# The feed-forward's down products read their activations in nine interleaved column orders

## The chip, the cores and the metric

The kernel runs on one core of a Trainium2 chip. The metric is the device time of one execution in microseconds (us). The engines are TensorE (PE in the profile; PEld is its weight load), VectorE (DVE), ScalarE (ACT), GpSimd (POOL) and SyncE (SP), which issues most DMAs. SBUF is the on-chip memory, PSUM the banks into which TensorE accumulates.

## The reference

A two-layer encoder over 512 positions of width 1024: each layer adds a mixer (attention heads in layer 0, an mLSTM in layer 1), a cross-attention to a memory, and a gated feed-forward with a short causal convolution. What bears on the change is the feed-forward:

```
def conv_ffn(xn, w_up, conv_w, conv_b, w_down):
    h = causal_depthwise_conv(xn @ w_up, conv_w) + conv_b
    g, u = jnp.split(h, 2, axis=-1)
    return (jax.nn.gelu(g) * u) @ w_down          # w_down: 2816 x 1024

x = x + conv_ffn(rms_norm(x, ffn_norm[layer]), ...)
```

Everything is float32.

## The kernel before, in words

x is kept transposed: eight tiles `x[m]` of 128 features x 512 positions, 4 bytes an element. A product with a weight matrix is cut into 128 x 128 weight blocks that are held in TensorE, past which the 512 columns (positions) of an activation tile are streamed. To keep float32 precision every operand is split into two fp32r parts, high and low, and each block is three matmuls, in `mm3` (lines 287 to 292): high by high (line 290), the activation's low part by the high weights (291), the high part by the low weights (292). So one "k" of a product is three weight loads and three matmuls of 512 columns. The first argument of `mm` after the bank is the held operand, the second the streamed one; in the profile's names the streamed one stands first behind the arrow (`w<-ah,wh` streams `ah` past weights of `wh`).

The feed-forward is `ffn_steps` (from line 1247). 2816 = 22 x 128 features go in 22 steps, "pairs" (gate and up half of one block): the first four as plain products (`plain`), the other 18 as seven products of half width (`seven`), in 256 columns. `tail` forms gate times up, and splits it into the activation tiles `acts[p]` = (`ah`, `al`), each 128 x 512, of which ten buffers exist. The down product is cut along its input features into five chunks, `CHUNKS`, of 4, 4, 4, 4 and 6 tiles (line 24). For chunk c and output block m, `down(c, m)` (line 1557) calls `block` (line 1310): it loads the weights, ScalarE and VectorE split them, TensorE runs 4 (or 6) times `mm3` into one of the two PSUM banks `w`, and VectorE adds the bank to `x[m]` (`xadd`, lines 615 to 618). So one block of chunks 0 to 3 is 12 matmuls, one of chunk 4 is 18. `block` also serves the plain up products, whose operand is `own` (line 1326).

The chunks' blocks are not run in one go: from pair 5 on, each pair calls `fill` twice, and each call takes one waiting block of down products. The last five blocks of chunk 3, and in layer 0 all of chunk 4, come after the last pair. In layer 1 chunk 4 is not run by `down` but in `finish` (line 1834), which does the final norm with it.

What order the instructions take on each engine is decided when the program is built, by `Sched`: every piece is added with an engine, an assumed duration, what it depends on, a due time and the buffers it takes (`raw`, `dr`: raw weights; `h`: split weights; `act`: ten activation tiles; `w`: two PSUM banks), and `Sched.run` places them. A `down` block is added to TensorE with 0.7 us for each k, its sum to VectorE with 0.6 us and 3 us later. The engines then run their fixed queues and wait for each other by semaphores.

The few lines that the change's steps touch, in `block` and in `down`:

```
for k in range(c * per, (c + 1) * per):
    self.mm3(st["ps"][:], *st["rows"](k), *xs(k), k == 0, k == nk - 1)
...
lambda k: tuple(a[:] for a in acts[first + k])
...
e = add("DVE", 0.6, lambda: self.xadd(m, d["ps"]), [last, xadded[m], *formed], clock[0] + 3.0, (), [("w", d)])
```

Of the kernel before, what the change touches and what calls it, by code (L numbers as in the profile page):

```python
# [13 lines left out]
ALU = mybir.AluOpType  # L14
# [50 lines left out]
class Plan:  # L65
# [11 lines left out]
    def add(self, fn, dur=0.0, deps=(), prio=None, take=(), free=(), chain=(), pre=(), after=0.0, order=(), load=(), st=None):  # L77
        it = Item(fn, dur, [d for d in deps if d is not None], len(self.items) if prio is None else prio, take, free, chain, pre, after, order, load, st)
        it.n = len(self.items)
        self.items.append(it)  # L80
        return it
# [67 lines left out]
class Sched:  # L149
# [22 lines left out]
    def run(self):  # L172
        order = sorted(self.tasks, key=lambda t: (t.prio, t.n))
        todo = {}
        want = {r: [] for r in self.slots}
        for t in order:
            todo.setdefault(t.eng, []).append(t)
        for t in self.tasks:
            for r, _ in t.take:
                want[r].append(t)  # L180
        now = {e: 0.0 for e in todo}
        inf = float("inf")
        idle = 0.0
        done = []
        while any(todo.values()):
            best = None
            for e, ts in todo.items():
                soon, pick = inf, None
                for t in ts[:120]:
                    at = 0.0 if e == "-" else now[e]  # L190
                    ok = True
                    for d in t.deps:
                        if d.end is None:
                            ok = False
                            break
                        at = max(at, d.end + (0.0 if d.eng == e else d.lat))
                    if not ok:
                        continue
                    for r, _ in t.take:
                        if want[r][0] is not t:  # L200
                            ok = False
                            break
                        at = max(at, self.slots[r][self.slot(r)])
                    if not ok or at == inf:
                        continue
                    if at < soon - 1e-6:
                        soon, pick = at, t
                if pick is not None and (best is None or soon < best[0]):
                    best = (soon, e, pick)
            assert best is not None, [(e, t.n, t.prio, [d.n for d in t.deps if d.end is None], t.take) for e, ts in todo.items() for t in ts[:3]]  # L210
            at, e, t = best
            todo[e].remove(t)
            if e == "PE":
                idle += at - now[e]
            t.start, t.end = at, at + t.dur
            now[e] = t.end
            for r, st in t.take:
                want[r].pop(0)
                s = self.slot(r)
                self.turn[r] += 1  # L220
                self.slots[r][s] = inf
                st["_" + r] = s
            for r, st in t.free:
                self.slots[r][st["_" + r]] = t.end + 0.1
            done.append(t)
        self.now, self.idle = now, idle
        products = [t for t in done if t.eng == "PE"]
        for a, b in zip(products, products[1:]):
            if a.block is not None and b.narrow:
                a.block["apart"] = a.block["step"]  # L230
        for t in done:
            if t.fn:
                t.fn()


class Builder:
# [185 lines left out]
    def xs(self):  # L422
        return self.xh, self.xl
# [188 lines left out]
            self.gained(k, self.x[k][:], self.col(gain, gi * 8 + k), self.xh[k][:], self.xl[k][:])  # L612
        self.squares(k, self.x[k][:], SEQ, state)

    def xadd(self, m, ps, reload=False):
        if reload:
            self.nc.sync.dma_start(self.x[m][:], self.t["x"][m])
        self.nc.vector.tensor_tensor(out=self.x[m][:], in0=ps[:], in1=self.x[m][:], op=ALU.add)  # L618


    def constants(self):
# [625 lines left out]
    def ffn_steps(self, layer, mp):  # L1247
# [3 lines left out]
        nc, t = self.nc, self.t  # L1251
        sc = Sched(raw=3, h=3, s2=1, s4=1, a22=1, sa=3, sb=2, ra=1, hs=2, c=1, dr=2, v=1, u2=1, u3=1, act=10, acc=4, s=2, w=2)
        add = sc.add
# [3 lines left out]
        clock = [0.0]  # L1257
        state = {}
        acts, acted = {}, {}
# [3 lines left out]
        def pe(dur, fn, deps, take=(), free=()):  # L1263
            clock[0] += dur
            return add("PE", dur, fn, deps, clock[0] - dur, take, free, 0.2)

        def joined(deps, prio, free):
            return add("-", 0.0, None, deps, prio, (), free, 0.0)
# [18 lines left out]
        def weight(src, cols, at, tag="raw", off=0):  # L1287

            st = {"apart": 0}
            l = load(st, tag, src, cols, at - 9.0)  # L1290

            def hi():
                st["wh"], st["wl"] = (self.til(self.wp, i, (P, 1088), F32R, bufs=3)[:, off:] for i in ("wh", "wl"))
                nc.scalar.copy(st["wh"][:, :cols], st[tag][:, :cols])  # L1294

            def low():
                n, end = st["apart"], cols - P
                for a, b, c in ((0, end, 0), (end, cols, n)) if n else ((0, cols, 0),):
                    self.sub(st["wl"][:, a + c : b + c], st[tag][:, a:b], st["wh"][:, a:b])

            def rows(k):
                s, n = slice(k * P, (k + 1) * P), k * P + (st["apart"] if (k + 1) * P == cols else 0)
                return st["wh"][:, s], st["wl"][:, n : n + P]

            st["rows"] = rows
            h = add("ACT", act(cols), hi, [l], at - 3.0, [("h", st)])
            lo = add("DVE", tt(cols), low, [h], at - 2.0, (), [(tag, st)])
            return st, lo

        def block(src, nk, xs, at, bank, deps, steps, tag="raw", off=0):  # L1310

            st, lo = weight(src, nk * P, at, tag, off)
            last = None
            per = nk // steps
            for c in range(steps):

                def fn(c=c):
                    if c == 0:
                        st["ps"] = self.acc_bank(st["_acc"]) if bank == "acc" else self.bank(bank)
                    for k in range(c * per, (c + 1) * per):  # L1320
                        self.mm3(st["ps"][:], *st["rows"](k), *xs(k), k == 0, k == nk - 1)

                last = pe(0.7 * per, fn, [lo, last, *deps], [(bank, st)] if c == 0 else (), [("h", st)] if c == steps - 1 else ())
            return st, last
# [33 lines left out]
        formed = []  # L1358
# [195 lines left out]
        xadded = [None] * 8  # L1554
        queue, late = [], []

        def down(c, m, steps=1):
            first, nk = CHUNKS[c]
            d, last = block(
                t[f"down{c}"][layer, m], nk, lambda k: tuple(a[:] for a in acts[first + k]), clock[0], "w", [acted[first + k] for k in range(nk)], steps,  # L1560
                "dr" if nk == 4 else "raw", OFF,
            )
            last.block, d["step"] = d, 16
            if m == 7:
                for k in range(nk):
                    joined([last], last.prio, [("act", acted[first + k].st)])
            e = add("DVE", 0.6, lambda: self.xadd(m, d["ps"]), [last, xadded[m], *formed], clock[0] + 3.0, (), [("w", d)])
            xadded[m] = e
            return e

        def fill():
            nonlocal queue
            if queue:
                down(*queue.pop(0))
# [15 lines left out]
        if layer == 0:  # L1590
            for m in range(8):
                e = down(4, m, 2)
                a = add("ACT", 1.2, lambda m=m: self.xprep(m, "mix", 1, state), [e], clock[0] + 3.0)
                add("DVE", 1.3, None, [a], clock[0] + 3.0)
# [419 lines left out]
```

## Time and profile before

| what | value |
|---|---|
| time, median of 2 runs | 1471.14 us (1469.96 to 1472.32) |
| profiled execution, first to last instruction (span) | 1468.1 us, 3.0 us under the median of the runs; it has no time of its own beside the span |
| TensorE busy | 1455.4 us, 99% |
| VectorE busy | 1225.7 us, 83% |
| ScalarE busy | 843.8 us, 57% |
| bytes moved by DMA | 179.15 MB, mean 122 GB/s |
| matmuls of the down products that the change touches (`w<-ah` and `w<-al`) | 3 x 304 |
| their sums into x (line 618, `x<-w,x`) | 72 |

How to read it: the page lists for each engine how long it was busy, then how busy it was along the span, then the chain of work that ended last, then groups of instructions by source line (line, engine, operation, tiles, shape, count, then busy us and mean ns of one, then idle time before them). A row of the view of busy time by window has, after the window's bounds and length, the busy time and the count of instructions for each engine, the granted TensorE clock, the DMA engines' busy share and GB/s. A row of the timeline has the start and the duration in us, the engine, line, operation, tiles, shape and count. A matmul's duration runs from its start until its last result is out, so matmuls overlap, and the step from one start to the next is the time that it occupies TensorE.

The down products lie at 467 to 747 us in layer 0 and at 1177 to 1424 us in layer 1.

### The profile page before, as it was taken

What the parts mean: (1) busy time and instruction counts of PE and PEld (TensorE: products, weight loads), DVE (VectorE), ACT (ScalarE), POOL (GpSimd) and SP (SyncE); (2) the same over time, 40 slices, a digit from 0 to 9 for tenths busy, and PEclk for the clock granted to TensorE, in tenths of its full rate; (3) what the DMA queues carried; (4) which work ended last, traced back from release to release, by engine and by line L of the source; (5) the groups of instructions that cost most, each with busy time, mean ns of one, the idle gap of its engine ahead of it and who ended that gap; (6) DMA issues with size and microseconds to landing.
All of it is one profiled execution on the core that took longest, in us unless ns stands there. A gap on an engine that the chain in (4) does not pass through costs nothing.

```text
span 1468.1 us, 22621 instructions
## 1 busy us (share of the span) xinstructions
PE 1455.4 (99%) x8503; PEld 1268.9 (86%) x8503; DVE 1225.7 (83%) x2246; ACT 843.8 (57%) x1425; POOL 63.1 (4%) x102
## 2 busy tenths in 40 slices
PE   9999999999999999999999999999999999999998
PEld 7888787888888999999888888888888899999987
DVE  7789985756589999999769988676557999999984
ACT  7788664544466555555457655354445655555554
POOL 0001120000000000000000100000000000000000
PEclk9999999999999999999999999999999999999999
DMA  5222433323237666562333332332323756655422
GB/s 198 87 73 73 122 120 118 115 92 109 86 130 194 166 156 168 157 159 76 92 99 108 115 101 76 119 102 99 115 87 115 191 156 163 161 165 153 118 67 77
DMA packets 64798, 179.15 MB, mean 122 GB/s; under 512 B 7072, under 2 KB 7072, under 8 KB 64688
## 3 DMA queue, kind: packets, MB, share of 16 engines
q1 hardware_dynamic: 58496, 157.71, 33.4%
q0 software_dynamic: 5184, 18.88, 7.7%
q8 instruction: 66, 1.08, 0.3%
q10 hardware_dynamic: 1008, 1.12, 0.2%
q14 instruction: 44, 0.36, 0.1%
HBM read 175.55 MB, written 2.13 MB: 121 GB/s over the span
## 4 chain that ended last, share of the span: by engine, by line
PE 78%; DVE 15%; ACT 3%; issue 2%; DMA 1%; SPq 0%; POOL 0%; ACTq 0%; DVEq 0%; POOLq 0%
PE acc L290 15%; PE acc L291 15%; PE acc L292 15%; PE w L292 5%; PE w L290 5%; PE w L291 5%; DVE wl L281 3%; PE s L290 2%; PE s L292 2%; PE s L291 2%; DVE c L1404 2%; PE acc L351 2%; PE acc L353 2%; PE acc L352 2%; DVE x L770 1%
## 5 line engine op out<-in xcount | busy, mean ns | idle before, releaser
L290 PE MATMUL acc<-xh,wh 128*128 128x512 f32 (+1 forms) x800 | 281.9, 352 | 0.1
L292 PE MATMUL acc<-xh,wl 128*128 128x512 f32 (+1 forms) x800 | 280.0, 350 | 1.1 <-DVE wl L281 1.1
L291 PE MATMUL acc<-xl,wh 128*128 128x512 f32 (+1 forms) x800 | 279.5, 349 | 0.0
L281 DVE TENSOR_TENSOR wl<-raw,wh 128x1024 fp32r<-128x1024 f32 (+4 forms) x199 | 235.7, 1185 | 27.1 <-ACT wh L284 22.9
L284 ACT CAST wh<-raw 128x1024 fp32r<-128x1024 f32 (+1 forms) x135 | 139.3, 1036 | 142.4 <-PE acc L291 89.8
L292 PEld LDWEIGHTS acc<-xh,wl 128*128 128x128 f32 x800 | 150.2, 188 | 22.2 <-DVE wl L281 2.0
L290 PEld LDWEIGHTS acc<-xh,wh 128*128 128x128 f32 x800 | 150.2, 188 | 20.2 <-ACT v L1643 0.6
L291 PEld LDWEIGHTS acc<-xl,wh 128*128 128x128 f32 x800 | 150.3, 188 | 19.7
L1404 DVE SCALAR_TENSOR_TENSOR c<-hs,vec,c 128x512 f32<-128x512 f32 x176 | 129.7, 743 | 0.9 <-ACT c L1397 0.8
L292 PE MATMUL w<-ah,wl 128*128 128x512 f32 x304 | 119.0, 391 | 0.0
L290 PE MATMUL w<-ah,wh 128*128 128x512 f32 x304 | 118.6, 390 | 0.0
L291 PE MATMUL w<-al,wh 128*128 128x512 f32 x304 | 118.6, 390 | 0.0
L1397 ACT ACTIVATE c<-hs,vec 128x512 f32<-128x512 f32 x88 | 69.4, 812 | 47.6 <-DVE hs L1547 34.6
L1294 ACT CAST wh<-dr 128x512 fp32r<-128x512 f32 x64 | 39.6, 619 | 55.7 <-PE w L291 20.5
L292 PEld LDWEIGHTS w<-ah,wl 128*128 128x128 f32 x304 | 57.1, 188 | 12.2
L290 PEld LDWEIGHTS w<-ah,wh 128*128 128x128 f32 x304 | 57.1, 188 | 10.4 <-ACT ah L1418 0.6
L291 PEld LDWEIGHTS w<-al,wh 128*128 128x128 f32 x304 | 57.1, 188 | 9.6
L618 DVE TENSOR_TENSOR x<-acc,x 128x512 f32<-128x512 f32 x32 | 22.0, 691 | 49.3 <-PE acc L292 49.3
L290 PE MATMUL acc<-mem,wh 128*128 128x256 f32 (+1 forms) x192 | 61.2, 319 | 0.0
L291 PE MATMUL acc<-mem,wh 128*128 128x256 f32 (+1 forms) x192 | 61.0, 318 | 0.0
L292 PE MATMUL acc<-mem,wl 128*128 128x256 f32 (+1 forms) x192 | 60.8, 317 | 0.0
L618 DVE TENSOR_TENSOR x<-w,x 128x512 f32<-128x512 f32 x72 | 49.2, 683 | 11.8 <-PE w L292 11.1
(469 smaller groups left out, 3992.4 us busy)
## 6 DMA issues: line engine op xcount, KB each, us to landing
raw<-in_up_dram SPq DMA_DIRECT2D x52, 512.0 KB, 3.3
sa<-in_up_dram SPq DMA_DIRECT2D x36, 512.0 KB, 4.4
sa<-in_up_dram POOLq DMA_DIRECT2D x36, 512.0 KB, 5.5
dr<-in_down_dram SPq DMA_DIRECT2D x64, 256.0 KB, 2.9
ra<-in_up_dram SPq DMA_DIRECT2D x36, 256.0 KB, 3.1
raw<-in_xk_dram SPq DMA_DIRECT2D x16, 512.0 KB, 3.4
raw<-in_wo_dram SPq DMA_DIRECT2D x16, 512.0 KB, 3.3
raw<-in_xq_dram SPq DMA_DIRECT2D x16, 512.0 KB, 3.3
```

What stands on the lines that cost most here:

```text
L281: self.nc.vector.tensor_tensor(out=lo, in0=v, in1=hi.bitcast(F32), op=ALU.subtract)
L284: self.nc.scalar.copy(hi, v)
L290: mm(out, wh, xh, start=first, stop=False, skip_group_check=parts)
L291: mm(out, wh, xl, start=False, stop=False, skip_group_check=parts)
L292: mm(out, wl, xh, start=False, stop=last, skip_group_check=parts)
L351: mm(ps, xh[k][:, ts], wh[:, ws], start=(k == 0), stop=False)
L352: mm(ps, xh[k][:, ts], wl[:, ws], start=False, stop=False)
L353: mm(ps, xl[k][:, ts], wh[:, ws], start=False, stop=(k == 7))
L618: self.nc.vector.tensor_tensor(out=self.x[m][:], in0=ps[:], in1=self.x[m][:], op=ALU.add)
L1294: nc.scalar.copy(st["wh"][:, :cols], st[tag][:, :cols])
L1397: nc.scalar.activation(st["c_"][:, j, :], hs()[:, j, 2:514], AF.Identity, scale=self.col("cw", (layer * 3 + 2) * 44 + blk), bias=self.col( ...
L1404: nc.vector.scalar_tensor_tensor(out=c, in0=hs()[:, j, n : n + 512], scalar=w, in1=c, op0=ALU.mult, op1=ALU.add)
```

## The change

For each layer and chunk an order (h, f) is given. It views the 512 columns as h parts of 512 / h, and streams f neighbouring columns from part 0, f from part 1, and so on through all h parts, then the next f from part 0. (2, 2) for instance streams columns 0, 1, 256, 257, 2, 3, 258, 259, and so on. The bank is written front to back in the order of the stream, so a bank's columns are in that order too. `xadd` reads the bank front to back and reads and writes x in the same interleaved order, so each sum lands where it did. Chunk 4 of layer 1, in `finish`, stays as it was; its entry (None) is not used.

Nine blocks of down products get an order, four or five in each layer:

| layer | chunk 0 | chunk 1 | chunk 2 | chunk 3 | chunk 4 |
|---|---|---|---|---|---|
| 0 | h 2, f 2 | h 2, f 4 | h 2, f 16 | h 4, f 16 | h 2, f 8 |
| 1 | h 8, f 16 | h 16, f 16 | h 4, f 8 | h 16, f 4 | as before |

The instructions of every engine, their order and their waits are the same as before; an operand of 912 matmuls and two operands of 72 additions are described by three steps where it was one.

```
+def woven(h, f):
+    return lambda a: a.rearrange("p (h c f) -> p c h f", h=h, f=f)
+
+ORDERS = [
+    [woven(2, 2), woven(2, 4), woven(2, 16), woven(4, 16), woven(2, 8)],
+    [woven(8, 16), woven(16, 16), woven(4, 8), woven(16, 4), None],
+]
...
-    def xadd(self, m, ps, reload=False):
+    def xadd(self, m, ps, reload=False, order=None):
         if reload:
             self.nc.sync.dma_start(self.x[m][:], self.t["x"][m])
-        self.nc.vector.tensor_tensor(out=self.x[m][:], in0=ps[:], in1=self.x[m][:], op=ALU.add)
+        x, ps = self.x[m][:], ps[:]
+        if order is not None:
+            x = order(x)
+            for n in reversed(x.shape[2:]):
+                ps = ps.rearrange("p (a b) -> p a b", b=n) if len(ps.shape) == 2 else ps.rearrange("p (a b) c -> p a b c", b=n)
+        self.nc.vector.tensor_tensor(out=x, in0=ps, in1=x, op=ALU.add)
...
                     for k in range(c * per, (c + 1) * per):
-                        self.mm3(st["ps"][:], *st["rows"](k), *xs(k), k == 0, k == nk - 1)
+                        x = xs(k)
+                        out = st["ps"][:]
+                        for n in reversed(x[0].shape[2:]):
+                            out = out.rearrange("p (a b) -> p a b", b=n) if len(out.shape) == 2 else out.rearrange("p (a b) c -> p a b c", b=n)
+                        self.mm3(out, *st["rows"](k), *x, k == 0, k == nk - 1)
...
             first, nk = CHUNKS[c]
+            order = ORDERS[layer][c]
             d, last = block(
-                t[f"down{c}"][layer, m], nk, lambda k: tuple(a[:] for a in acts[first + k]), clock[0], "w", [acted[first + k] for k in range(nk)], steps,
+                t[f"down{c}"][layer, m], nk, lambda k: tuple(order(a[:]) for a in acts[first + k]), clock[0], "w", [acted[first + k] for k in range(nk)], steps,
                 "dr" if nk == 4 else "raw", OFF,
             )
...
-            e = add("DVE", 0.6, lambda: self.xadd(m, d["ps"]), [last, xadded[m], *formed], clock[0] + 3.0, (), [("w", d)])
+            e = add("DVE", 0.6, lambda: self.xadd(m, d["ps"], order=order), [last, xadded[m], *formed], clock[0] + 3.0, (), [("w", d)])
```

## The prediction

> **What bounds the kernel now.** I read the page first: the span, the busy shares and the granted clock. Then I read the busy times by window for the feed-forward stages, the waits of TensorE there, and the timeline for the step from one matmul to the next.
>
> ```profile
> span 1468.1 us, 22621 instructions
> PE 1455.4 (99%) x8503; PEld 1268.9 (86%) x8503; DVE 1225.7 (83%) x2246; ACT 843.8 (57%) x1425; POOL 63.1 (4%) x102
> PEclk9999999999999999999999999999999999999999
> PE 78%; DVE 15%; ACT 3%; issue 2%; DMA 1%; SPq 0%; POOL 0%; ACTq 0%; DVEq 0%; POOLq 0%
> ```
>
> TensorE is busy from end to end at the full granted clock. The chain that ended last runs mostly through it. The 15% on VectorE warns that a second engine is close, so I look at the stages that the change touches: 440 to 700 us and 1150 to 1430 us (the pairs of layer 0 and 1, with the early down products between them), and 700 to 760 us (the late down products of layer 0).
>
> ```profile
> core 0: us, PE busy (x) PEld busy (x) DVE busy (x) ACT busy (x) POOL busy (x), PEclk, DMA share, GB/s
> 440.00:700.00 260.00, 259.29 (x1875) 242.27 (x1874) 258.12 (x436) 148.46 (x232) 14.64 (x18) 1.00 0.59 153
> 700.00:760.00 60.00, 59.93 (x275) 49.25 (x274) 43.83 (x66) 28.88 (x42) 0.10 (x1) 1.00 0.31 95
> 1150.00:1430.00 280.00, 279.27 (x1972) 258.86 (x1971) 274.80 (x461) 158.67 (x247) 14.73 (x18) 1.00 0.56 148
> PE acc L290 <- DVE u L1523: 0.2, 1, 0.2
> ```
>
> TensorE is idle for 0.7 us of 260, and the only wait of TensorE's matmuls that the view of waits lists between 460 and 700 us is the last row, 0.2 us. VectorE is idle for 1.9 us of 260 and 5.2 us of 280. So in these stages TensorE ends last and VectorE stands right behind it: time added to a down product has nothing to hide in, and time added to a sum on VectorE has some 7 us at most.
>
> **What one down product costs.** A matmul's duration includes its way through the array; what counts is the step from start to start.
>
> ```profile
> 703.48:747.20 43.72, 43.71 (x192) 35.95 (x193) 7.53 (x11) 0.00 (x0) 1.00 0.30 92
> L290 PE MATMUL w<-ah,wh 128*128 128x512 f32 x304 | 118.6, 390 | 0.0
> L291 PE MATMUL w<-al,wh 128*128 128x512 f32 x304 | 118.6, 390 | 0.0
> L292 PE MATMUL w<-ah,wl 128*128 128x512 f32 x304 | 119.0, 391 | 0.0
> ```
>
> The first row is a window over the tile w: 192 matmuls of the late down products, back to back, in 43.72 us. That is 43.72 / 192 = 0.2277 us for 512 columns, or 0.445 ns a column, although each lasts 0.39. The other rows count the matmuls that change: 3 x 304 = 912, in all 912 x 0.2277 = 208 us of TensorE.
>
> **The change, part by part.** Nothing is added or removed: the same instructions stand on every engine in the same order with the same waits, no DMA moves, and the planner's costs are the same numbers. What differs is one operand of 912 matmuls (the moving one; the output bank is still written front to back) and two operands of 72 sums. An order (h, f) cuts the 512 columns into h equal parts and takes f neighbours from each in turn. So the stream is made of runs of f columns with a jump between them. By run length: runs of 2 in layer 0's chunk 0 (8 blocks x 4 k x 3 = 96 matmuls); of 4 in layer 0's chunk 1 and layer 1's chunk 3 (192); of 8 in layer 0's chunk 4 and layer 1's chunk 2 (144 + 96 = 240); of 16 in the other four (384). Together 912.
>
> *The moving operand.* No matmul of this trace streams a jumping operand, so its price has to be bounded. Lower end: nothing, since 512 columns already go at one steady pace, and no row shows a faster one; for a gain I leave 10 us below (912 x 0.011, a twentieth of the step), because no row excludes that a stream with jumps meets fewer collisions with the weight loads beside it. Upper end: the slowest steady stream of 4-byte columns in the trace, the transposes.
>
> ```profile
> L1215 PE MATMUL w<-ident,xe 128*128 128x128 f32 x64 | 10.5, 272 | 0.0
> 287.57 0.60 PE L1215 MATMUL w<-ident,xe 128*128 128x128 f32 x4
> ```
>
> Four of them take 0.60 us, the last 0.272 of it in flight, so the step is (0.60 - 0.272) / 3 = 0.109 us for 128 columns, 0.855 ns a column. A 512-column product at that pace takes 0.438 us, 0.210 more than now. For all 912 that is +191.5 us.
>
> Between these ends the run length decides. The nearest rows that jump at all are VectorE's, when it forms the gate weights in runs of 4 and 8 columns:
>
> ```profile
> L281 DVE TENSOR_TENSOR wh<-gw,wh 128x32 fp32r<-128x32 f32 x2 | 0.3, 188 | 0.0
> L281 DVE TENSOR_TENSOR wh<-gw,wh 128x64 fp32r<-128x64 f32 x1 | 0.2, 215 | 0.0
> L281 DVE TENSOR_TENSOR wl<-dr,wh 128x128 fp32r<-128x128 f32 x56 | 15.8, 283 | 0.0
> L281 DVE TENSOR_TENSOR al<-c,ah 128x512 fp32r<-128x512 f32 x44 | 30.1, 683 | 0.2
> ```
>
> Without jumps, 128 to 512 columns cost (683 - 283) / 384 = 1.04 ns a column, so 32 would take 183 ns and 64 would take 216. With runs of 4 and 8 they take 188 and 215. So VectorE finds a new run every 4 x 1.04 = 4.2 ns at next to no cost. At TensorE's present pace runs of 16 come every 7.1 ns and runs of 8 every 3.6: about what that row shows, and I take nothing for them. Runs of 4 come every 1.78 ns, runs of 2 every 0.89, beyond what any row shows. If a run can be had as often as a pair of columns in the slow stream (2 x 0.855 = 1.71 ns), runs of 4 just keep pace and runs of 2 fall to 0.855 ns a column. That is my choice: runs of 4 nothing, runs of 2 the upper end, 96 x 0.210 = **+20.2 us**. The ends I keep are 0 and +191.5.
>
> [...]
>
> *The sums.* 72 additions into x read and write x in runs.
>
> ```profile
> L618 DVE TENSOR_TENSOR x<-w,x 128x512 f32<-128x512 f32 x72 | 49.2, 683 | 11.8 <-PE w L292 11.1
> ```
>
> They cost what the contiguous subtraction above costs (683 ns), so they are at the plain pace. Lower end: nothing, as in the gate rows. Upper end: the 5 ns that 8 runs of 4 took too long there, 0.63 ns a run: 8 x 256 + 16 x 128 + 16 x 64 + 32 x 32 = 6144 runs, 3.9 us in all, behind the 7 us that VectorE has idle. I take nothing. If that cover is gone, the 3.9 us go into the span. A sum that ends later frees its w bank later (two banks), which would hold the next but one block.
>
> *What follows a slower product.* In layer 0's chunk 0 (the first 96, from 467.65 us on) each block of 12 takes 2.5 us longer. Behind it on TensorE stand the seven products of a pair; ScalarE and VectorE then wait a little more for banks, but gain the slack that they lack now. DMAs are at 0.59 of the engines' time and ask for nothing more.
>
> **Sum.** 1468.1 + 20.2 = 1488.3 us of span. The runs' median is 1471.14, 3.0 us above the profiled span, so the forecast is **1491 us**, 1.4% slower. A difference of about 2%, or 29 us, is what a measurement of this kernel can tell from no change.
>
> **Rivals.**
> - *No price at all* (1471 us). For: VectorE's gate rows jump free. Against: they run at less than half TensorE's pace. [...]
> - *Every jump costs one column's time*, in the address stepping, whatever the run. Runs: 96 x 256 + 192 x 128 + 240 x 64 + 384 x 32 = 76,800, times 0.445 ns = +34.2 us: 1505, slower by 2.3%, the other side of my forecast. It decides from 0.38 ns a jump on (29.4 us / 76,800). For: TensorE has no slack for it. Against: the 0.63 ns a run of the gate rows, if it is more than scatter, was VectorE's, and 64 columns in runs of 8 showed none.
> - *Runs of 4 pay as well* (start addresses, or two parts that collide): 288 x 0.210 = +60.5 us, 1532.
> - *Any interleaved stream falls to the slow pace*: +191.5, 1663. For: the transposes show that a 4-byte stream can go that slowly. Against: runs of 16 jump every 7 ns only.
> - *The sums pay, not the products*: at twice the plain pace each sum takes 512 x 1.04 = 0.53 us more. Some 59 of them lie in the two full stages, 31 us, less VectorE's 7 us idle: +24, 1495.
> - *A small gain* through fewer collisions: 1461.
>
> **How the numbers follow.** Forecast 0.30, no price 0.25, a price per jump 0.13, runs of 4 too 0.08, everything slow 0.13, sums 0.05, gain 0.06. I predict the likeliest, 1491; its own range is 1483 to 1498, since part of an added 20 us could fall into waits and runs of 2 could be a little better or worse than the transposes. The range is 1460 to 1550: it leaves out the case in which everything is slow (0.13) and some 0.05 of odd outcomes. Slower by over 2%: 0.13 + 0.08 + 0.10 of the price per jump + 0.03 of the forecast's upper tail = 0.34. Faster by over 2%: 0.01, as 29 us of the 208 would need a column in 0.38 ns. Within 2%: 0.65.
>
> **What would show it.** In the changed profile, layer 0's chunk 0 (from 467.65 us on) should have steps of about 0.44 us, and all other down products 0.228; the late ones from about 724 us on should again take 43.7 us for 192. L618's successor should stay at 683 ns. The forecast is wrong if the first 96 step at 0.228 (no price), if steps grow with the number of jumps (0.228 + 0.114, 0.057, 0.028, 0.014 for runs of 2, 4, 8, 16: a price per jump), if runs of 4 or of 16 go at 0.44, or if the sums lengthen.

## The result and the profile after

The changed kernel takes 1489.97 us (median of 2 runs, 1489.52 to 1490.42) against 1471.14 before: a ratio of 1.0129, 95% interval 1.0099 to 1.0158. It is slower, by 1.3%; the forecast was 1491.

The page of the changed kernel, the lines that answer to those shown of before:

```profile
span 1487.5 us, 22621 instructions
PE 1474.9 (99%) x8503; PEld 1272.6 (86%) x8503; DVE 1227.9 (83%) x2246; ACT 843.8 (57%) x1425; POOL 62.4 (4%) x102
PEclk9999999999999999999999999999999999999999
PE 82%; DVE 12%; ACT 3%; issue 2%; DMA 1%; POOL 0%; SPq 0%; ACTq 0%; DVEq 0%; POOLq 0%
L635 DVE TENSOR_TENSOR x<-w,x 128x512 f32<-128x512 f32 x72 | 49.2, 684 | 16.2 <-PE w L304 15.8
```

TensorE's busy time grew by 19.5 us and the span by 19.4. The clock is the same (0.999 in both), VectorE's busy time grew by 2.2 us, and the sums (now line 635) take 684 ns where they took 683. So the time went to TensorE, and the chain shifts from VectorE to it. The busy time by window over the tile w shows where. A row is one block of down products between its first start and the next product's start; first the kernel before, plain order, then the changed one with one block of each order (layer 0's chunks 0 to 3, layer 1's chunks 0 to 3), then the same late 192 matmuls as in the prediction's window.

```profile
471.76:474.50 2.74, 2.74 (x12) 2.07 (x12) 0.68 (x1) 0.00 (x0) 1.00 0.93 215
```

```profile
473.73:477.73 4.00, 4.00 (x12) 2.15 (x12) 0.00 (x0) 0.00 (x0) 1.00 0.11 44
545.79:548.81 3.02, 3.02 (x12) 2.08 (x12) 0.00 (x0) 0.00 (x0) 1.00 0.79 199
602.43:605.31 2.88, 2.88 (x12) 2.09 (x12) 0.00 (x0) 0.00 (x0) 1.00 0.38 124
671.71:674.51 2.80, 2.80 (x12) 2.07 (x12) 0.00 (x0) 0.00 (x0) 1.00 0.97 167
1197.01:1199.87 2.86, 2.86 (x12) 2.08 (x12) 0.68 (x1) 0.00 (x0) 1.00 0.49 138
1270.91:1273.79 2.88, 2.88 (x12) 2.08 (x12) 0.00 (x0) 0.00 (x0) 1.00 0.68 176
1323.33:1326.10 2.77, 2.77 (x12) 2.07 (x12) 0.00 (x0) 0.00 (x0) 1.00 0.65 189
1390.79:1393.74 2.95, 2.95 (x12) 2.11 (x12) 0.00 (x0) 0.00 (x0) 1.00 0.18 65
716.57:762.85 46.28, 46.27 (x192) 36.33 (x193) 7.53 (x11) 0.00 (x0) 1.00 0.29 88
```

Every order costs something, and none costs what the forecast gave it. A plain block takes 2.74 us. The extra time of the one block that is shown, times the eight blocks of its chunk:

| order | run | extra per block, us | chunk, us | forecast, us |
|---|---|---|---|---|
| (2,2) | 2 | 1.26 | 10.1 | 20.2 |
| (2,4), (16,4) | 4 | 0.28, 0.21 | 2.2 + 1.7 | 0 |
| (2,8), (4,8) | 8 | 0.29 (18 matmuls), 0.03 | 2.3 + 0.2 | 0 |
| (2,16), (4,16), (8,16), (16,16) | 16 | 0.14, 0.06, 0.12, 0.14 | 1.1 + 0.5 + 1.0 + 1.1 | 0 |
| all | | | 20.2 | 20.2 |

For (2,8) the late window is used: 46.28 - 43.72 = 2.56 us, less 4 blocks of (4,16), 0.24 us, leaves 2.3 us for its eight blocks. The table goes by one block of each kind; the steps of all 912 matmuls, added up, grew by 19.7 us, 10.1 of it in the runs of 2 and 9.6 in the other eight orders. So the total was met because two errors cancel: runs of 2 pay half of the forecast, the other eight orders pay the other half.

### The profile page after: what moved, and what is told of

Its sections match the earlier page's. It is cut to its first block, busy times and chain, and to the rows that moved or that the text cites. A ratio compares the mean times of both kernels' runs of the same rounds, so it can differ in the third digit from the quotient of the medians.

```text
span 1487.5 us, 22621 instructions
## 1 busy us (share of the span) xinstructions
PE 1474.9 (99%) x8503; PEld 1272.6 (86%) x8503; DVE 1227.9 (83%) x2246; ACT 843.8 (57%) x1425; POOL 62.4 (4%) x102
## 4 chain that ended last, share of the span: by engine, by line
PE 82%; DVE 12%; ACT 3%; issue 2%; DMA 1%; POOL 0%; SPq 0%; ACTq 0%; DVEq 0%; POOLq 0%
PE acc L302 16%; PE acc L303 16%; PE acc L304 16%; PE w L303 6%; PE w L304 6%; PE w L302 6%; PE s L302 3%; PE s L304 3%; PE s L303 3%; DVE wl L293 2%; PE acc L363 2%; PE acc L365 2%; PE acc L364 2%; DVE c L1425 2%; PE w L816 1%
## 5 line engine op out<-in xcount | busy, mean ns | idle before, releaser
L303 PE MATMUL w<-al,wh 128*128 128x512 f32 x304 | 126.1, 415 | 0.0
L304 PE MATMUL w<-ah,wl 128*128 128x512 f32 x304 | 126.0, 414 | 0.0
L302 PE MATMUL w<-ah,wh 128*128 128x512 f32 x304 | 125.8, 414 | 0.0
```

What stands on the lines that cost most here:

```text
L302: mm(out, wh, xh, start=first, stop=False, skip_group_check=parts)
L303: mm(out, wh, xl, start=False, stop=False, skip_group_check=parts)
L304: mm(out, wl, xh, start=False, stop=last, skip_group_check=parts)
```

## The experiments

Theory J, from the table alone, is a fixed slot for each jump (1.26 us / 12 / 256 jumps = 0.41 ns). It fits (2,2), (2,16), (8,16) and (16,16), and fails for runs of 4 and 8. The rivals are named where they come up.

**Eight orders without the first.** Chunk 0 of layer 0 goes back to plain order.

```
-    [woven(2, 2), woven(2, 4), ...
+    [None, woven(2, 4), ...
```

> The changed kernel with layer 0's chunk 0, runs of 2, put back to plain order in products and sums; the other eight orders stay. If the forecast's step was right (runs of 2 carry all of the price) this is the kernel before: 1471 us. If the changed kernel's own steps are right, runs of 2 carry 96 x 0.106 = 10 us and the others the rest: 1480 us.

Measured: 1479.62 us, ratio to before 1.0065 (1.0047 to 1.0083). Runs of 2 carry 1489.97 - 1479.62 = 10.4 us by the medians and 1487.5 - 1477.8 = 9.7 by the profiled spans, and the other eight orders 8 to 10. The forecast's step is wrong, the reading of the blocks right.

**Only the sums.** The products stream in plain order, the sums stay interleaved: layer 0 with the change's orders, layer 1 with single columns. What the layers compute on is thereby permuted.

```
-  lambda k: tuple(order(a[:]) for a in acts[first + k])
+  lambda k: tuple(a[:] for a in acts[first + k])
-    [woven(8, 16), woven(16, 16), woven(4, 8), woven(16, 4), None],
+    [woven(2, 1), woven(256, 1), woven(128, 1), woven(16, 1), None],
```

> Only the sums are interleaved, the products stream their columns front to back as before; so the sums land in permuted columns of x, and the layers compute on permuted sums. Layer 0 has the five orders of the change; layer 1 has single columns: (2,1), (256,1), (128,1), (16,1). If the change's whole price lies in the products: step 0.227 us throughout, layer 0's sums at 0.684 us, the layer 0 part as before. If the sums carry any of it: layer 0's part longer by up to 20 us. [...]

The view of the sums by window, layer 0 whole, then a stretch of layer 1 with (256,1) alone:

```profile
440.00:760.00 320.00, 27.37 (x40) 1.00 0.53 142
1250.00:1300.00 50.00, 4.85 (x7) 1.00 0.63 168
```

40 sums in layer 0's orders take 27.37 us, 0.684 each: free, as forecast. The four orders of layer 1 were not run alone; with products and sums in them, the changed kernel's sums there take 0.684 us. With (256,1), steps of two columns, a sum takes 0.69 us. With the other orders of single columns it takes 1.1 to 1.2 us, where a sum in plain order takes 0.68. The span was 1475.1 us, so 24 dear sums (some 10 us of VectorE) brought 7: VectorE's thin cover in these stages is real.

**The tiles 32 bytes further.** Theory P says that crossing a 64-byte piece of the row costs.

```
+  self.pad(mp, 32)
   act_()
-  self.pad(mp, 192)
+  self.pad(mp, 160)
```

> The changed kernel, with the activation tiles 32 bytes further along in SBUF: as built they start 32 bytes past a multiple of 64, here on one. Theory J (each jump costs the same slot, 0.106 us / 256 = 0.41 ns, wherever it lands): nothing moves, steps stay at 0.333, 0.252, 0.240, 0.233, 0.243 us in layer 0 and 0.238, 0.240, 0.231, 0.246 in layer 1, span 1487.5 us. Theory P (what costs is passing from one 64-byte piece of a row to another; runs of 16 columns are 64 bytes and straddle two pieces as the tiles lie): the four orders with runs of 16 fall to 0.227, that is 96 x (0.013 + 0.006 + 0.011 + 0.013) = 4 us less, span 1483.4, runs of 2, 4 and 8 unchanged. Theory W (the stream collides with the weight loads beside it, by the relative place of the two): prices of all orders change, in no order of run length.

The mean steps stayed: (2,16) 0.240, (4,16) 0.234, (8,16) 0.238, (16,16) 0.240 us, as before the shift. P falls. W is not borne out either: no order's mean step moved by more than 4 ns, and (2,16) later cost 0.240 us in another chunk. The span was 1491.7 us, 4 longer, spread over the pairs of both layers; this is from a single profile, and its cause stays open.

**Other orders, and single columns.**

```
-    [woven(2, 2), woven(2, 4), woven(2, 16), woven(4, 16), woven(2, 8)],
-    [woven(8, 16), woven(16, 16), woven(4, 8), woven(16, 4), None],
+    [woven(4, 2), woven(8, 2), woven(16, 2), woven(4, 4), woven(8, 4)],
+    [woven(8, 8), woven(16, 8), woven(2, 16), woven(2, 2), None],
```

> Other orders in products and sums: layer 0 (4,2), (8,2), (16,2), (4,4), (8,4); layer 1 (8,8), (16,8), (2,16), (2,2). If the price belongs to the order and not to its chunk, (2,2) costs 0.333 and (2,16) 0.240 us a matmul in layer 1 as they did in layer 0. Theory J (run length alone, priced by the change's own rows): all runs of 2 at 0.333, runs of 4 at 0.25, runs of 8 at 0.24; 384 x 0.106 + 240 x 0.025 + 192 x 0.015 + 96 x 0.013 = 51 us, span 1519. Theory D (the distance of the jump counts too; h = 4, 512 bytes, was the cheap one twice): (4,2) and (4,4) at about half the price, 0.28 and 0.237 us, h = 8 and 16 like h = 2; span about 1512.

Blocks of (4,2), (8,2), (16,2), and of (2,2) in layer 1:

```profile
474.79:480.17 5.38, 5.38 (x12) 2.25 (x12) 0.00 (x0) 0.00 (x0) 1.00 0.16 42
573.79:579.69 5.90, 5.90 (x12) 2.28 (x12) 0.00 (x0) 0.00 (x0) 1.00 0.20 48
637.99:643.53 5.54, 5.54 (x12) 2.29 (x12) 0.00 (x0) 0.00 (x0) 1.00 0.48 139
1456.36:1460.36 4.00, 4.00 (x12) 2.14 (x12) 0.00 (x0) 0.00 (x0) 1.00 0.11 13
```

(2,2) takes 4.00 us a block in another layer too: the price belongs to the order, not to its place. But other runs of 2 cost 0.45 to 0.49 us a matmul, about the 0.438 that the forecast had taken from the transposes, and far from J's 0.333. Theory D falls as well: (4,2) and (4,4) take 0.448 and 0.268 us a matmul, where it had 0.28 and 0.237. The span was 1559.9 us.

> Products stream single columns with jumps: layer 0 (2,1), (256,1), (128,1), (64,1), (8,1); layer 1 (32,1), (16,1), (4,1), and (4,16) as a control. The sums are plain, so they land in permuted columns of x. Theory J (0.41 ns a jump): 512 jumps, 0.440 us for every order of single columns, 816 x 0.213 = 174 us, span 1642. [...] A stream limited by fetches, one per run of 2 every 0.333/256 = 1.30 ns: 512 x 1.30 = 0.666 us, 816 x 0.44 = 358 us, span 1826. Control (4,16) 0.233.

The edit is the same with orders of single columns and plain sums. Blocks of (2,1), (256,1), (128,1), (64,1) and (4,1):

```profile
471.36:473.94 2.58, 2.58 (x12) 2.08 (x12) 0.68 (x1) 0.00 (x0) 1.00 1.03 170
550.12:555.54 5.42, 5.42 (x12) 2.27 (x12) 0.00 (x0) 0.00 (x0) 1.00 0.15 58
633.15:638.65 5.50, 5.50 (x12) 2.27 (x12) 0.00 (x0) 0.00 (x0) 1.00 0.47 143
704.16:709.32 5.16, 5.16 (x12) 2.26 (x12) 0.00 (x0) 0.00 (x0) 1.00 0.72 181
1457.35:1460.63 3.28, 3.28 (x12) 2.09 (x12) 0.00 (x0) 0.00 (x0) 1.00 0.26 94
```

This was the surprise of the study, and it ends J: (2,1), with a jump at every column, takes 2.58 us a block, 0.216 a matmul, *less* than plain order. And (256,1), which only steps by two columns, takes 5.42 us, twice as long. The other orders of single columns but (4,1) take 0.430 to 0.487 us a matmul. The control (4,16) stayed at 0.234. The span was 1613.9 us, 28 below J's.

Theory T answers to (2,1) and (256,1). It is about the order alone: call the even places of the stream one lane and the odd places the other; then the pace goes by how each lane steps, not by where the two lie. In (2,1) the even lane walks column by column through the first half and the odd lane through the second: 0.216 us a matmul. In plain order each lane steps by two, 0.227 us, in (256,1) by four, 0.452 us. What in TensorE would do this no row shows.

**Pairs at any distance.** If T holds, how far apart the two lanes walk should not count. The walks leave columns out or take them twice.

```
+def walk(*dims):                      # (step, count) of each loop, the innermost last
+    return lambda a: bass.AP(a.tensor, a.offset, [a.ap[0], *[list(d) for d in dims]])
+def pair_at(d):
+    return walk((1, 256), (d, 2))      # columns c, c + d, c + 1, c + 1 + d, ...
```

> Products stream pairs (column c, column c + d), c = 0 to 255: in layer 0 d = 128, 64, 16, 4, 0; in layer 1 d = 1, then even columns of the first half with odd columns of the second in turn (each lane steps two columns), then d = 252, then d = 256 as in (2,1). Where d is not 256 columns are left out or taken twice, and the sums are plain, so what is computed is not the feed-forward's product; only the steps are read. Theory T (two lanes, each with neighbours): 0.216 us for every d, and about 0.227 for the lanes that step two columns. Theory H (the two places of a pair have to lie 1024 bytes apart, in different halves): 0.216 for d = 256 only, 0.43 to 0.49 like the single columns of the earlier run for d = 128, 64, 16, 4. Theory J (each jump its slot): 0.44 for all.

Blocks with d = 128, then d = 1, then two lanes that step by two columns in different places:

```profile
472.06:474.65 2.59, 2.59 (x12) 2.08 (x12) 0.69 (x1) 0.00 (x0) 1.00 0.73 172
1178.04:1180.63 2.59, 2.59 (x12) 2.08 (x12) 0.68 (x1) 0.00 (x0) 1.00 0.96 164
1256.75:1259.50 2.75, 2.75 (x12) 2.07 (x12) 0.00 (x0) 0.00 (x0) 1.00 0.86 231
```

All distances give 0.216 (0, 4, 16, 64, 252 and 256 too), and two lanes that step by two in different places go at plain order's 0.227. T stands, H and J fall.

**A price by pieces.** Plain order and steps of four suggest a way to count. Cut the row into pieces of four columns: in plain order each lane passes 128 of them, at 0.2267 us / 128 = 1.77 ns a piece, and in (256,1) each passes 256, at 0.452 us / 256, again 1.77 ns. The estimate from these two steps and that of (2,1): a matmul takes the larger of 0.216 us and 1.77 ns times the pieces that one lane passes. With lanes that take r neighbouring columns and then skip r, that is 0.227 us for r = 2 and 0.216 from r = 4 on; with steps of three columns, 192 pieces, 0.340; with steps of six, 256 pieces, 0.453 and not more than with steps of four.

```
+def lanes(r):
+    return walk((2 * r, 256 // r), (1, r), (r, 2))      # each lane r neighbours, then skips r
+ORDERS = [
+    [lanes(2), lanes(4), lanes(8), lanes(32), walk((0, 2), (3, 128), (64, 2))],
+    [walk((0, 4), (6, 64), (64, 2)), walk((0, 2), (2, 128), (0, 2)), walk((2, 128), (128, 2), (1, 2)), walk((2, 128), (248, 2), (1, 2)), None],
+]
```

> Only steps are read; the sums are plain, and most walks leave columns out or take them twice. [...] Rival J: a jump costs the stream a slot of 0.41 ns: local runs of 2, 4, 8, 32: 0.333, 0.27, 0.24, 0.222.

Blocks of the lanes in runs of 2 and of 4; of lanes that step by six columns; of runs of 2 from two places 512 and 992 bytes apart:

```profile
471.91:474.65 2.74, 2.74 (x12) 2.07 (x12) 0.68 (x1) 0.00 (x0) 1.00 0.51 138
550.72:553.31 2.59, 2.59 (x12) 2.08 (x12) 0.00 (x0) 0.00 (x0) 1.00 0.75 221
1199.10:1204.51 5.41, 5.41 (x12) 2.27 (x12) 0.00 (x0) 0.00 (x0) 1.00 0.18 43
1343.70:1347.70 4.00, 4.00 (x12) 2.15 (x12) 0.00 (x0) 0.00 (x0) 1.00 0.39 131
1420.68:1424.62 3.94, 3.94 (x12) 2.14 (x12) 0.00 (x0) 0.00 (x0) 1.00 0.08 12
```

0.227 and 0.216 for runs of 2 and 4 as T had it (and 0.216 for 8 and 32); 0.451 for steps of six; for steps of three, 192 pieces, 142 of its 143 measured steps lie within 1 ns of 0.340, as T had it. J's values for the local runs did not come. Runs of 2 from *two* places take 0.328 to 0.333 at three distances: counted T's way, a lane that changes to and fro between two pieces pays 1.30 ns a piece, not 1.77. Nor is that a fixed price: in (4,1) each lane also goes to and fro between two places, at every column of its own, and its 0.273 us are 1.07 ns a change. T is no exact rule for the other single columns either; it gives 0.453 for all of them, and they took 0.430 to 0.487.

**What is left.** For runs of 4 to 16 T gives 128 pieces a lane and so plain order's 0.227, but they cost 0.231 to 0.252 in the change, and up to 0.278 among the other orders. A last map, with walks of the same run lengths and other pitches:

```
+    [walk((0, 2), (8, 64), (1, 4)), walk((0, 4), (16, 32), (1, 4)), walk((0, 8), (32, 16), (1, 4)), walk((0, 32), (128, 4), (1, 4)), walk((0, 2), (32, 16), (1, 16))],
+    [walk((0, 2), (16, 32), (1, 8)), walk((0, 16), (256, 2), (1, 16)), walk((0, 16), (128, 4), (1, 8)), walk((0, 32), (256, 2), (1, 8)), None],
```

> [...] Only steps are read; the sums are plain and the walks leave columns out and repeat others. Runs of 4 at a pitch of 8, 16, 32 columns and over four places 128 apart in turn; runs of 16 at a pitch of 32; in layer 1 runs of 8 at a pitch of 16, runs of 16 from two places 256 apart in turn, runs of 8 from four places 128 apart in turn, runs of 8 from two places 256 apart in turn. Rival A (any jump costs a little, since the next piece is not the neighbour of the last): runs of 4 about 0.25 us, runs of 8 about 0.24, runs of 16 about 0.237 throughout. Rival B (only a stream that comes back to earlier places pays): 0.227 for the walks that only go forward with a pitch, the price for those in turn. Rival C (the distance decides, not the run): no common value at one run length.

Mean steps: runs of 4 at pitch 8, 16, 32: 0.232, 0.236, 0.255; over four places in turn 0.287. Runs of 8 at pitch 16: 0.234; in turn 0.279. Runs of 16 at pitch 32: 0.240; in turn 0.242. Forward walks pay too (B falls), and one run length has no common price (A falls): for runs of 4 the pitch counts, as C had it, but by a rule that these runs don't give.

**The fast order put to use.** First in the down products alone: (2,1) in the products; the sum reads its bank with a step of two, and x stays plain.

```
+  x, ps = x.rearrange("p (h c) -> p h c", h=2), ps.rearrange("p (c h) -> p h c", h=2)
   self.nc.vector.tensor_tensor(out=x, in0=ps, in1=x, op=ALU.add)
```

> The kernel before, with every down product outside the final one streaming single columns from the two halves in turn, (2,1), the order that ran at 0.216 us a matmul in the single-column run; the bank is in that order, and the sum reads it with a step of two columns while x is read and written front to back. [...] The sums: 0.70 us if a step of two costs as in x with (256,1), 1.1 us if the bank is worse, then slower than before by some 20 us. If (2,1) was fast in the earlier run only by its chunk: 0.227 and no gain.

Measured: 1464.98 us, ratio 0.9961 (0.9947 to 0.9975). The matmuls step at 0.216 us in all nine chunks, and the sums take 680 ns with the step of two in the bank. The steps of the 912 matmuls add up to 10.1 us less, and 5.6 us of it arrive in the median.

Then the same order in nearly all products with split operands, their readers stepping by two:

```
+nat = lambda a: a.rearrange("p (h c) -> p h c", h=2)
+unw = lambda ps: ps.rearrange("p (c h) -> p h c", h=2)
+sw = lambda a: a.rearrange("p (h c) -> p c h", h=2)
+def mm3w(self, out, wh, wl, xh, xl, first, last, parts=False):
+    self.mm3(out.rearrange("p (c h) -> p c h", h=2), wh, wl, sw(xh), sw(xl), first, last, parts)
...
-  out=tq[:], in0=ps[:], scalar=-0.125, in1=self.rb,
+  out=nat(tq[:]), in0=unw(ps[:]), scalar=-0.125, in1=nat(self.rb),
```

> The order (2,1) in nearly all products with split operands: mixers' and cross-attention's projections, plain and seven feed-forward products (256 wide, so halves 512 bytes apart), down products, the first five final blocks; every reader of their banks steps by two. Theory T: 0.216 us for 512 columns and about 0.108 for 256; some 2000 matmuls of 512 columns outside the down products, 2000 x 0.011 = 22 us, on top of the 5.6 us of the down products alone; the seven products' 3024 x 0.0057 = 17 us only as far as VectorE, full there, lets through. 1428 to 1444 us. If bank reads with a step of two are dear on ScalarE or VectorE: up to 20 us less gain.

Measured: 1447.71 us (1445.73 to 1449.55), ratio 0.9847 (0.9832 to 0.9863): faster than both kernels, though 4 us above the range that was expected. Its page and its windows over the pairs of the two layers (TensorE, weight loads, VectorE, ScalarE, GpSimd):

```profile
span 1445.5 us, 22635 instructions
PE 58%; DVE 32%; issue 4%; ACT 4%; DMA 1%; POOL 0%; SPq 0%; DVEq 0%; POOLq 0%; ACTq 0%
430.00:690.00 260.00, 255.71 (x1880) 240.08 (x1879) 259.30 (x439) 149.78 (x233) 15.52 (x18) 1.00 0.58 154
1140.00:1410.00 270.00, 265.55 (x1936) 248.77 (x1935) 265.19 (x448) 153.90 (x241) 13.68 (x16) 1.00 0.55 147
```

VectorE's share of the chain went from 15% to 32%, and in the first stage it is idle for 0.7 us of 260 while TensorE is idle for 4.3. The view of TensorE's waits puts 3.4 of their 4.1 us in that window on VectorE, which is now the bound there. But the seven products had little to give: their 256 columns step at 0.112 us, where 0.113 was the pace before and 0.108 was expected, and with the waits between them their 3024 steps add up to 355.0 us against 350.1. From the first down product to the last, layer 0 is 3.7 us shorter than before and layer 1 2.7, hardly more than with the down products alone (3.5 and 2.1). Most of the gain lies outside these stages, where other products of 512 columns now step at 0.216.

## Why the prediction was right, and where it was not

- *The total.* Met by luck: one term came out at half of its size, and what was put at nothing made up the other half.
- *The bound and the cover.* Right: no slack on TensorE. The products' extra 19.7 us, over all their steps, appear as 19.4 of span.
- *The sums are free.* Right: 684 ns against 683, and layer 0's alone cost nothing. The gate rows, runs of 4 and 8 at the plain pace, were the right evidence.
- *Runs of 2: +20.2 us.* The step that failed in size: 10.1 us by the blocks, 9.7 to 10.4 by taking the order away. The price was borrowed from the transposes' pace (0.109 us for 128 columns, so 0.438 for 512). That row need not show a slow stream, for in the kernel before products of only 2 columns are about as slow. The first row has eight of them, the second the product that follows:

```profile
836.47 0.95 PE L451 MATMUL s<-ones,hsq 128*128 128x2 f32 x8
837.28 0.49 PE L351 MATMUL acc<-wh,xh 128*128 128x512 f32 x1
```

The eight take 837.28 - 836.47 = 0.81 us, 0.10 each, and 28 of the 32 in the trace step at 0.111 to 0.112. So what limits the transposes need not be their columns. Nor was 0.438 an upper end: three other orders with runs of 2 cost 0.45 to 0.49. But (2,2) has only two places to go to and fro between, and that is cheaper, 0.333, as are the runs of 2 from two places at other distances. The forecast priced the run length and did not ask for the number of places.
- *Runs of 4, 8 and 16: nothing.* Failed: 9.6 us together, 0.002 to 0.022 us a matmul. The argument was that VectorE finds a new run every 4.2 ns for nothing. But plain order is not TensorE's best pace (0.227 us, where (2,1) takes 0.216). That a disturbance has nothing to hide in at that pace is the author's estimate and was not shown; T itself gives these runs no price. VectorE's rows could not answer for TensorE: they go at 1.04 ns a column, less than half its pace (0.445 ns).
- *The rivals.* The price per jump had the runs of 2 nearly right (0.114 us a matmul, measured 0.106) and was right that every order pays, but there is not one price: 23 of its 34 us would have been on the eight other orders, which cost 10. By the signs that the prediction set itself, the first 96 matmuls, at 0.334 us, speak for this rival (0.228 + 0.114 = 0.342) and not for the forecast (0.44). The small gain was judged by the change's orders, and none of those is faster; the margin of 0.011 us below equals the distance to the fast order by luck.

What stays open: what in TensorE makes the even and the odd places of the stream count apart (T is read from the steps alone); why to and fro between two pieces costs 1.30 ns in (2,2), 1.07 in (4,1) and not 1.77; and by what rule of distance runs of 4 to 16 pay.

## What to carry to other kernels

A total that comes out right does not show that its terms are: read one block of each kind before believing the sum. Before taking a row as the pace of a stream, look for a row with far fewer columns that is as slow. Before pricing a disturbance, ask whether the undisturbed stream is already at a limit, by comparing its pace with the best that the engine shows anywhere. Streaming 4-byte columns as pairs from two halves of a tile, and reading the bank back with a step of two, took 5% off each such matmul of 512 columns here (0.227 to 0.216 us) and 1% off those of 256 (0.113 to 0.112), until VectorE became the bound, idle for 0.7 us of 260.

## What the runs showed of the hardware that was not expected

- TensorE streams 512 fp32r columns in 0.227 us front to back, and in 0.216 us when even and odd places each walk column by column, at any of the distances tried between them (0 to 256 columns). For 256 columns the two are 0.113 and 0.112 us, and products of 2 columns step at 0.111 to 0.112.
- The same stream takes 0.340 us when even and odd places each walk in steps of three columns, and no more in steps of six (0.451 us) than in steps of four (0.452 us).
- VectorE reads a PSUM bank, or reads and writes x, with a step of two columns at its plain pace (0.68 and 0.69 us), but needs 1.1 to 1.2 us a sum when x is taken in single columns that lie further apart.
